# Hybrid SSD and S5 block: two token tiles scaled before a plain transpose, and two weight splits put behind them

## The chip, the cores and the metric

The kernel runs on one core of a Trainium2 chip. The metric is device time in microseconds (us) of one execution, lower is better. The kernel before takes 818.63 us (median of 3 runs, 818.24 to 820.31). The core has a matrix engine (TensorE, PE in the profile; PEld is its weight load), VectorE (DVE), ScalarE (ACT), GpSimd (POOL) and a queue engine that issues most transfers (SyncE, SP). Each engine works through its own list in order; they wait for each other on semaphores.

## The reference

One decoder block in float32 over 512 tokens with 16 learned tokens put in front (528 tokens, width 1024). What matters here is its beginning:

```python
h = jnp.concatenate([meta, x], axis=1)          # 528 x 1024
n = _rmsnorm(h, g_mix[layer])                   # h * rsqrt(mean(h*h) + eps) * g
proj = n @ w_in[layer]                          # z, xbc, dt and u side by side
...
u = proj[..., o_u:]                             # the S5 mixer's input, 1024 columns
y_s5 = _s5_mixer(u, ...)
```

Behind it follow the SSD mixer, the S5 mixer, an output projection, a squared-ReLU MLP and a last norm.

## The kernel before, in words

**Precision.** Each matrix product is made of three products of split operands: a value is cast to a short form (`whi`, `xhi`, ScalarE) and the rest is kept as a second short value (`wlo`, `xlo`). `mm_cols` (L139) runs 24 matmuls for one weight of 128 columns: for each of the 8 blocks of 128 rows of the weight, `whi`·`xhi`, `whi`·`xlo` and `wlo`·`xhi`.

**The start.** The 528 tokens come as 16 learned ones and four tiles of 128 (`xt`, t = 0 to 3). `norm_transpose_split` handles one tile: ScalarE squares and sums a row (L149), VectorE and GpSimd make `rstd` (L150, L152), and TensorE turns the tile round so that features lie on partitions. It does this with eight ordinary float32 matmuls whose moving operand is a diagonal matrix of `rstd` (`diag`, L170 and L174), so that norm and turn are one step. VectorE multiplies each half of the turned tile (four blocks, h = 0 and 1) by the gain (L176), ScalarE casts it (`xhi`, L179) and VectorE subtracts (`xlo`, L180). A small ring of three buffers (`xgs`) carries the halves between these steps.

**The first products.** `u_split(f)` splits the weight of the f-th 128 columns of u, `u_half(f, i)` multiplies it with the first (i = 0) or second half of the tokens, 264 tokens each. The first half of the tokens is the 16 learned ones, tile 0 and all but 8 tokens of tile 1. `dt_half` does the same for 16 further columns (`pd`, L271). For f = 0 and 2 VectorE makes `wlo` (L118). For f = 1 ScalarE writes the negative of the weight (L121), and a transfer that GpSimd issues adds the weight onto it (L122), before ScalarE casts `whi` (L123). Three raw buffers and three pairs of split buffers go round, so the split for f = 3 starts when the second product of f = 0 is done.

**Behind it.** ScalarE copies the turned S5 constants (`lcol`, L306), from which VectorE works out exponentials and angles in a long string of small instructions; then come the S5 blocks, the SSD chunks, the projections and the MLP. The MLP works in four quarters of 28 units; a unit of its first product is one of seven named products (P1 to P7, `Quarter.up`), several of which share a bank of accumulators (`UP_BANK`, L1070: P1, P6, P7 and P4 use bank X).

**What sets the order.** The kernel is written as a sequence of calls; a scheduler orders them on each engine by a simulated time line, by data dependences and by priorities (weights are loaded and split with a high priority). A change at one place can therefore exchange neighbours at another.

Of the kernel before, what the change touches and what calls it, by code (L numbers as in the profile page):

```python
# [10 lines left out]
F32 = mybir.dt.float32  # L11
# [3 lines left out]
ALU = mybir.AluOpType  # L15
# [3 lines left out]
P = 128  # L19
SEQ = 512  # L20
NM = 16
# [17 lines left out]
AHEAD = 3000  # L39
# [6 lines left out]
def bc(ap, axis, n):  # L46
    a = ap.unsqueeze(axis)
    shape = list(a.shape)
    shape[axis] = n
    return a.broadcast_to(shape)  # L50
# [3 lines left out]
def hybrid_block_kernel(ctx, tc, x, meta_tokens, g_mix, w_in, conv_w, conv_b, dt_bias, a_log, d_ssd,  # L54
                        g_ssd, lam_re, lam_im, log_step, b_re, b_im, c_re, c_im, d_s5, w_glu, b_glu,
                        g_s5, w_out, g_mlp, w_up, w_down, g_final, out, dbg=None):
    nc = tc.nc
    V, A, G, T = nc.vector, nc.scalar, nc.gpsimd, nc.tensor
# [20 lines left out]
    def bank(name, dt=F32):  # L79
        tag = KIND.get(name, "x")  # L80
        return ps.tile([P, 512], dt, tag=tag, name=name, bufs=TAGS[tag])

    def slot(name, shape, dt=F32):
        return big.tile(shape, dt, tag="slot", name=name)


    ident = const.tile([P, P], F32, name="ident")
# [21 lines left out]
    def split_weight(raw, lo_engine=None, ahead=AHEAD, room=None):  # L109
        with (tc.high_priority(offset=ahead) if ahead else nullcontext()):  # L110
            if room is None:
                hi = wp.tile(list(raw.shape), F32R, tag="hi", name="whi", bufs=3)
                lo = wp.tile(list(raw.shape), F32R, tag="lo", name="wlo", bufs=3)
            else:
                hi, lo = room("whi", list(raw.shape)), room("wlo", list(raw.shape))
            if lo_engine is V:
                A.copy(hi, raw)  # L117
                V.tensor_tensor(out=lo, in0=raw, in1=hi.bitcast(F32), op=ALU.subtract)  # L118
            else:

                A.mul(lo, raw, -1.0)  # L121
                G.dma_start(out=lo.bitcast(F32), in_=raw, accum_op=ALU.add)  # L122
                A.copy(hi, raw)  # L123
        return hi, lo

    def load_cols(w, c0, n=P, ahead=AHEAD):
        return load_weight(w[:, c0:c0 + n].rearrange("(k p) c -> p k c", p=P), KD, n, ahead)
# [18 lines left out]
    def rstd_of(src, n, name):  # L146
        junk = scr[:, 3]
        v = mid.tile([P, 1], F32, tag="ssq", name="ssq")
        A.activation(out=junk[:n], in_=src, func=AF.Square, accum_out=v[:n])  # L149
        V.tensor_scalar(out=v[:n], in0=v[:n], scalar1=1.0 / DM, scalar2=EPS, op0=ALU.mult, op1=ALU.add)  # L150
        r = mid.tile([P, 1], F32, tag="rstd", name=name)
        last_pow.append(G.tensor_tensor(out=r[:n], in0=v[:n], in1=mhalf[:n, 0:1], op=ALU.pow))  # L152
        return r
# [8 lines left out]
            A.copy(hi, src_p)  # L162
            V.tensor_tensor(out=xlo[:, 4 * h:4 * h + 4, c0:c0 + n], in0=src_p, in1=hi.bitcast(F32), op=ALU.subtract)

    def norm_transpose_split(src, n, gcol, xhi, xlo, c0):

        r = rstd_of(src, n, "rstd")
        m = next(turn) % 3
        diag = scr[:, 1, 640 + m * P:640 + (m + 1) * P]
        last_xn.append(A.mul(diag[:n, :n], ident[:n, :n], r[:n, 0:1]))  # L170
        for h in range(2):
            pt = bank("pt")
            for k in range(4):
                T.matmul(pt[:, k * n:(k + 1) * n], lhsT=src[:, (4 * h + k) * P:(4 * h + k + 1) * P], rhs=diag[:n, :n])  # L174
            xg = xgs[:, next(xturn) % 3, 0:4 * n].rearrange("p (k n) -> p k n", k=4)
            V.tensor_tensor(out=xg, in0=pt[:, 0:4 * n].rearrange("p (k n) -> p k n", k=4),  # L176
                            in1=bc(gcol[:, 4 * h:4 * h + 4], 2, n), op=ALU.mult)
            hi = xhi[:, 4 * h:4 * h + 4, c0:c0 + n]
            A.copy(hi, xg)  # L179
            V.tensor_tensor(out=xlo[:, 4 * h:4 * h + 4, c0:c0 + n], in0=xg, in1=hi.bitcast(F32), op=ALU.subtract)  # L180

    s5_ctx = tc.tile_pool(name="s5", bufs=1)
    s5 = s5_ctx.__enter__()
    scr = slot("scr", [P, 4, DM])
    mt = scr[0:NM, 2]
    xgs = scr[:, 0:2].rearrange("p a (h c) -> p (a h) c", h=2)
    turn, xturn = itertools.count(), itertools.count()
    last_pow, last_xn = [], []
    xt = slot("xt", [P, 4, DM])
    xhi = slot("xhi", [P, KD, L], F32R)  # L190
    xlo = slot("xlo", [P, KD, L], F32R)
# [16 lines left out]
    gcol = const.tile([P, KD], F32, name="gcol")  # L208
# [37 lines left out]
    uw, uts = {}, {}  # L246

    def u_split(f):
        raw = first_raw[f] if f in first_raw else load_cols(w_in[0], O_U + f * P)
        uw[f] = split_weight(raw, V if f in (0, 2) else G, 0 if f < 3 else AHEAD)  # L250
        uts[f] = s5.tile([P, TS5, NC5], F32, tag="ut", name="ut", bufs=2)

    def u_half(f, i):
        pu = bank("pu")
        mm_cols(pu[:, 0:LH], uw[f], xx, P, halves[i])
        A.copy(uts[f][:, :, 66 * i:66 * i + 66], pu[:, 0:LH].rearrange("p (c t) -> p t c", t=TS5))
        if i == 1:
            dma2(out=Ud[f], in_=uts[f])
# [14 lines left out]
        return A.copy(dtT[:, halves[i]], pd[0:2 * NH, 0:LH])  # L273

    def prepare(t):
        norm_transpose_split(xt[:, t], P, gcol, xhi, xlo, NM + t * P)

    norm_transpose_split(mt, NM, gcol, xhi, xlo, 0)
    prepare(0)
    u_split(0)  # L280
    prepare(1)
    prepare(2)
    u_half(0, 0)
    prepare(3)
    u_split(1)
    u_half(1, 0)
    dt_split()
    dt_half(0)
# [145 lines left out]
    for part, (x0, x1, op) in enumerate(((bRt, bIt, ALU.subtract), (bIt, bRt, ALU.add))):  # L434
# [3 lines left out]
                        in1=tb2.rearrange("p (b j) h -> p b j h", b=8), op=op)  # L438
# [10 lines left out]
        A.copy(WW[:, :, fam, 2], WW[:, :, fam, 0])  # L449

    for f in range(2, 8):
        u_split(f)
        for i in range(2):
            u_half(f, i)

# [231 lines left out]
    def xbc_tile(f):  # L687
        return xcr[:, f] if f < 8 else bcr[:, f - 8]
# [22 lines left out]
    for n, f in enumerate(order):  # L711
        raw = xbc_tile(f)
# [22 lines left out]
    for ch in range(NCH):  # L735
        n = NM if ch == 0 else P
# [15 lines left out]
        if ch > 0:  # L752
# [20 lines left out]
            for h in range(2):  # L773
# [8 lines left out]
                for r in range(4):  # L782
# [6 lines left out]
                                op=ALU.mult)  # L789
# [134 lines left out]
    for f in range(8):  # L924
        A.activation(out=yhi[:, f], in_=xc[:, f, NM:L], func=AF.Copy, scale=col("gssd", f))
        V.scalar_tensor_tensor(out=ylo[f // 2][:, f % 2], in0=xc[:, f, NM:L], scalar=col("gssd", f),
                               in1=yhi[:, f].bitcast(F32), op0=ALU.mult, op1=ALU.subtract)
# [522 lines left out]
```

## Time and profile before

| what | value |
|---|---|
| median of 3 runs | 818.63 us |
| profiled execution, its own time | 819.08 us |
| its span, first to last instruction | 817.4 us |
| TensorE busy | 774.6 us, 95% of the span |
| VectorE busy | 625.9 us, 77% |
| ScalarE busy | 496.3 us, 61% |
| GpSimd busy | 75.5 us, 9% |

The rows of a time line give the start of an instruction and its length in us, the engine, the line of the kernel, the operation, out<-in by the names of the program, partitions x elements, a count where rows are merged, and in brackets how long the engine stood idle before it and what ended that. Rows of a table of stretches give, for a stretch A:B, the busy time and instructions of each engine, then the clock that TensorE was granted, the share of the transfer engines, and GB/s. One float32 matmul of a tile's turn shows as two records. Durations overlap a little: the spacing of starts is what one instruction costs in a sequence.

### The profile page before, as it was taken

Reading aid. Unit: us, or ns where it says so; the run is one execution under the profiler, and the core shown is the slowest. Engines: PE = TensorE matmul, PEld = TensorE weight load, DVE = VectorE, ACT = ScalarE, POOL = GpSimd, SP = SyncE. Lnnn points to the kernel's source line nnn. Section 1 sums busy time; section 2 is a strip of 40 time slices with the busy share of each in tenths; the row PEclk is TensorE's granted clock in tenths of the full one; section 3 lists DMA queues with packets and bytes.
Section 4 is the critical chain, followed back from the end, with each engine's and each line's share of the span. In section 5 each row is a group of like instructions: output and inputs, shape, how many; then the busy total and the mean of one; then the engine's idle time right before and its main releaser. Section 6 shows DMA issues by size and latency. Waiting matters only on the chain. (4 is left out here: it accounts for less than half of the span.)

```text
span 817.4 us, 12922 instructions
## 1 busy us (share of the span) xinstructions
PE 774.6 (95%) x4943; PEld 682.0 (83%) x4943; DVE 625.9 (77%) x972; ACT 496.3 (61%) x782; POOL 75.5 (9%) x125
## 2 busy tenths in 40 slices
PE   6999899999999999989999989999999999999996
PEld 6999898998787778768888879878997899789975
DVE  4489798998785779769534588698679867987897
ACT  7578798988544753555123475654665466546665
POOL 3211000011000110010100000100010001000101
PEclk9999999999999999999999999999999999999998
DMA  9999575768664654344335028864485448654622
GB/s 242 194 232 217 113 167 138 172 141 190 144 154 133 163 131 132 104 125 160 123 103 186 21 78 244 192 155 156 129 181 155 156 130 181 180 159 112 117 51 104
DMA packets 129638, 121.90 MB, mean 149 GB/s; under 512 B 21836, under 2 KB 105720, under 8 KB 129576
## 3 DMA queue, kind: packets, MB, share of 16 engines
q1 hardware_dynamic: 121224, 90.66, 37.7%
q0 software_dynamic: 8352, 30.41, 20.4%
q8 instruction: 39, 0.64, 0.3%
q14 instruction: 23, 0.19, 0.1%
HBM read 83.76 MB, written 6.88 MB: 111 GB/s over the span
## 5 line engine op out<-in xcount | busy, mean ns | idle before, releaser
L997 DVE TENSOR_TENSOR wlo<-quad,whi 128x1024 fp32r<-128x1024 f32 x40 | 49.0, 1224 | 37.1 <-ACT whi L1012 34.5
L1232 PE MATMUL u<-opC,whi 128*128 128x256 f32 x384 | 71.5, 288 | 3.0 <-DVE r L99 2.0
L1012 ACT CAST whi<-quad 128x1024 fp32r<-128x1024 f32 x40 | 41.9, 1048 | 49.3 <-DMA quad<-raw 17.3
L1273 PE MATMUL acc<-whi,al 128*128 128x512 f32 x160 | 63.4, 396 | 3.7 <-DVE al L997 3.7
L1232 PEld LDWEIGHTS u<-opC,whi 128*128 128x128 f32 x384 | 60.6, 195 | 4.6 <-DVE r L99 2.6
L117 ACT CAST whi<-raw 128x1024 fp32r<-128x1024 f32 x31 | 32.3, 1043 | 52.6 <-PE acc L837 31.6
L118 DVE TENSOR_TENSOR wlo<-raw,whi 128x1024 fp32r<-128x1024 f32 x31 | 37.9, 1222 | 31.8 <-ACT whi L117 31.2
L1273 PE MATMUL acc<-whi,ah 128*128 128x512 f32 x160 | 59.6, 393 | 1.4 <-ACT ah L1012 1.4
L1273 PE MATMUL acc<-wlo,ah 128*128 128x512 f32 x160 | 60.3, 390 | 0.0
L139 PE MATMUL pxb<-xhi,whi 128*128 128x264 f32 x192 | 55.3, 288 | 1.6 <-ACT xcr L695 1.6
L139 PE MATMUL pxb<-xhi,wlo 128*128 128x264 f32 x192 | 55.8, 291 | 0.0
L139 PE MATMUL pxb<-xlo,whi 128*128 128x264 f32 x192 | 55.5, 289 | 0.0
L1232 PE MATMUL u<-opC,wlo 128*128 128x256 f32 x192 | 54.0, 286 | 0.0
L1012 ACT CAST whi<-bquad 128x1024 fp32r<-128x1024 f32 x34 | 35.7, 1049 | 30.0 <-PE acc L1273 20.8
L1232 PE MATMUL u<-opB,whi 128*128 128x256 f32 x256 | 48.6, 288 | 1.2 <-DVE opB L997 1.2
L1232 PE MATMUL u<-opA,whi 128*128 128x256 f32 x256 | 46.7, 280 | 0.2 <-ACT whi L1012 0.2
L997 DVE TENSOR_TENSOR wlo<-bquad,whi 128x1024 fp32r<-128x1024 f32 x34 | 41.5, 1221 | 3.2 <-ACT whi L1012 3.2
L1232 PEld LDWEIGHTS u<-opB,whi 128*128 128x128 f32 x256 | 40.8, 194 | 1.6 <-DVE opB L997 1.4
L1273 PEld LDWEIGHTS acc<-whi,al 128*128 128x128 f32 x160 | 30.0, 188 | 13.4 <-DVE al L997 7.5
L1232 PEld LDWEIGHTS u<-opA,whi 128*128 128x128 f32 x256 | 39.5, 188 | 0.6 <-ACT whi L1012 0.4
L1232 PE MATMUL u<-opB,wlo 128*128 128x256 f32 x128 | 37.1, 290 | 2.4 <-DVE wlo L997 2.4
L122 POOL DMA_DIRECT2D wlo<-raw x26 | 22.3, 856 | 179.2 <-ACT xcr L695 62.0
(435 smaller groups left out, 2429.0 us busy)
## 6 DMA issues: line engine op xcount, KB each, us to landing
raw<-in_w_in_dram SPq DMA_DIRECT2D x28, 512.0 KB, 4.2
wlo<-raw POOLq DMA_DIRECT2D x26, 512.0 KB, 5.2
raw<-in_w_up_dram SPq DMA_DIRECT2D x22, 512.0 KB, 4.2
raw<-in_w_glu_dram SPq DMA_DIRECT2D x16, 512.0 KB, 4.0
raw<-in_w_out_dram SPq DMA_DIRECT2D x16, 512.0 KB, 4.2
bquad<-in_w_down_dram SPq DMA_DIRECT2D x16, 512.0 KB, 3.6
quads<-in_w_down_dram SPq DMA_DIRECT2D x16, 512.0 KB, 4.4
bquad<-quads POOLq DMA_DIRECT2D x16, 512.0 KB, 5.1
```

The costliest lines, as they stand in the source:

```text
L117: A.copy(hi, raw)
L118: V.tensor_tensor(out=lo, in0=raw, in1=hi.bitcast(F32), op=ALU.subtract)
L122: G.dma_start(out=lo.bitcast(F32), in_=raw, accum_op=ALU.add)
L139: T.matmul(ps_out, lhsT=w[a][:, k, 0:m], rhs=x[b][:, k, tok], start=(n == 0), stop=(n == len(steps) - 1))
L997: V.tensor_tensor(out=out, in0=a, in1=b, op=ALU.subtract)
L1012: A.copy(hi, src)
L1232: T.matmul(pb[:, mm], lhsT=w[a][:, k, mm * P:(mm + 1) * P], rhs=x[:, b, k], start=(first and n == 0), stop=(n in (11, 23)), skip_group_che ...
L1273: T.matmul(banks[s], lhsT=at[x][:, g, j, s * P:(s + 1) * P], rhs=wt[y][:, j], start=(fresh and g == 0 and j == 0 and k == 0), stop=(g == 1 ...
```

## The change

Tiles 0 and 1 are scaled in place by ScalarE (`A.mul(src, src, r)`, 128 x 1024), and turned by TensorE's plain transpose with the identity. The learned tokens and tiles 2 and 3 keep the diagonal matrix. The second weight (f = 1) gets its low part from VectorE instead of from the transfer. The splits of f = 1 and of f = 2 to 7 are ordered behind the last parts (`xhi` and `xlo` of h = 1) of tile 1.

```diff
-    def norm_transpose_split(src, n, gcol, xhi, xlo, c0):
+    def norm_transpose_split(src, n, gcol, xhi, xlo, c0, scaled=False):
         r = rstd_of(src, n, "rstd")
-        m = next(turn) % 3
-        diag = scr[:, 1, 640 + m * P:640 + (m + 1) * P]
-        last_xn.append(A.mul(diag[:n, :n], ident[:n, :n], r[:n, 0:1]))
+        if scaled:
+            last_xn.append(A.mul(src, src, r[:n, 0:1]))
+        else:
+            m = next(turn) % 3
+            diag = scr[:, 1, 640 + m * P:640 + (m + 1) * P]
+            last_xn.append(A.mul(diag[:n, :n], ident[:n, :n], r[:n, 0:1]))
         for h in range(2):
             pt = bank("pt")
             for k in range(4):
+                if scaled:
+                    T.transpose(pt[:, k * n:(k + 1) * n], src[:, (4 * h + k) * P:(4 * h + k + 1) * P], ident[:n, :n])
+                    continue
                 T.matmul(pt[:, k * n:(k + 1) * n], lhsT=src[:, (4 * h + k) * P:(4 * h + k + 1) * P], rhs=diag[:n, :n])
...
-            A.copy(hi, xg)
-            V.tensor_tensor(out=xlo[:, 4 * h:4 * h + 4, c0:c0 + n], in0=xg, in1=hi.bitcast(F32), op=ALU.subtract)
+            last_parts[:] = [A.copy(hi, xg),
+                             V.tensor_tensor(out=xlo[:, 4 * h:4 * h + 4, c0:c0 + n], in0=xg, in1=hi.bitcast(F32),
+                                             op=ALU.subtract)]
...
-        uw[f] = split_weight(raw, V if f in (0, 2) else G, 0 if f < 3 else AHEAD)
+        uw[f] = split_weight(raw, V if f < 3 else G, 0 if f < 3 else AHEAD)
...
-        norm_transpose_split(xt[:, t], P, gcol, xhi, xlo, NM + t * P)
+        norm_transpose_split(xt[:, t], P, gcol, xhi, xlo, NM + t * P, scaled=t < 2)
...
     prepare(1)
+    second = list(last_parts)
     prepare(2)
     u_half(0, 0)
     prepare(3)
-    u_split(1)
+
+    with tc.issue_after(second[0].ins), tc.issue_after(second[1].ins):
+        u_split(1)
...
     for f in range(2, 8):
-        u_split(f)
+        with tc.issue_after(second[0].ins), tc.issue_after(second[1].ins):
+            u_split(f)
```

How the lists of the engines move is seen at three places. The first is ScalarE at the start, from the square of tile 1 on; before:

```order
L149 ACTIVATE scr,ssq<-xt 128x1024
L170 ACTIVATE scr<-ident,rstd 128x128
L117 CAST whi<-raw 128x1024
L170 ACTIVATE scr<-ident,rstd 128x128
L179 CAST xhi<-scr 128x4x16
L149 ACTIVATE scr,ssq<-xt 128x1024
L179 CAST xhi<-scr 128x4x16
L121 ACTIVATE wlo<-raw 128x1024
L123 CAST whi<-raw 128x1024
L170 ACTIVATE scr<-ident,rstd 128x128
L117 CAST whi<-raw 128x1024
L179 CAST xhi<-scr 128x4x128
```

and with the change:

```order
L149 ACTIVATE scr,ssq<-xt 128x1024
L170 ACTIVATE xt<-xt,rstd 128x1024
L117 CAST whi<-raw 128x1024
L170 ACTIVATE xt<-xt,rstd 128x1024
L186 CAST xhi<-scr 128x4x16
L149 ACTIVATE scr,ssq<-xt 128x1024
L186 CAST xhi<-scr 128x4x16
L186 CAST xhi<-scr 128x4x128
L174 ACTIVATE scr<-ident,rstd 128x128
L186 CAST xhi<-scr 128x4x128
L149 ACTIVATE scr,ssq<-xt 128x1024
L186 CAST xhi<-scr 128x4x128
```

Two diagonals became two scalings of a whole tile, and the three instructions on the weights of f = 1 and 2 left this place; the casts of tile 0 come in their stead.

The second is VectorE at the same time, from the first half of tile 0 (`scr<-pt` with 512 elements is the gain); before, and then with the change:

```order
L176 TENSOR_TENSOR scr<-pt,gcol 128x512 x2
L118 TENSOR_TENSOR wlo<-raw,whi 128x1024
L301 COPY lrow<-lsr 32x128
L180 TENSOR_TENSOR xlo<-scr,xhi 128x4x128
L176 TENSOR_TENSOR scr<-pt,gcol 128x512
L150 TENSOR_SCALAR ssq<-ssq 128x1
L266 TENSOR_TENSOR wdt_parts<-scr,wdt_parts 128x8x16
L176 TENSOR_TENSOR scr<-pt,gcol 128x512
L180 TENSOR_TENSOR xlo<-scr,xhi 128x4x128 x2
```

```order
L183 TENSOR_TENSOR scr<-pt,gcol 128x512 x2
L187 TENSOR_TENSOR xlo<-scr,xhi 128x4x128
L312 COPY lrow<-lsr 32x128
L150 TENSOR_SCALAR ssq<-ssq 128x1
L183 TENSOR_TENSOR scr<-pt,gcol 128x512
L187 TENSOR_TENSOR xlo<-scr,xhi 128x4x128
L274 TENSOR_TENSOR wdt_parts<-scr,wdt_parts 128x8x16
L187 TENSOR_TENSOR xlo<-scr,xhi 128x4x128
L183 TENSOR_TENSOR scr<-pt,gcol 128x512
L118 TENSOR_TENSOR wlo<-raw,whi 128x1024 x2
```

In the second piece the first two gains are those of tile 1; tile 0's gains and its first `xlo` stand ahead of it. The low part of one weight stood between tile 0's gains and its `xlo`; now the low parts of two weights stand behind the whole of tile 1.

The third is far from the edit: ScalarE in the first quarter of the MLP, about 495 us into the span. Before, and then with the change (`r<-u` copies an accumulator bank: L1242 and its later number L1254 is P5, L1244 and L1256 is P6; `r<-r` with two instructions is a squared ReLU):

```order
L1244 COPY r<-u 128x2x256
L1012 CAST whi<-quad 128x1024
L1073 ACTIVATE r<-r 128x2x256
L1074 ACTIVATE r<-r 128x2x256
L1012 CAST whi<-quad 128x1024
L1073 ACTIVATE r<-r 128x2x256
L1074 ACTIVATE r<-r 128x2x256
L1073 ACTIVATE r<-r 128x2x256
L1074 ACTIVATE r<-r 128x2x256
L1012 CAST whi<-quad 128x1024
L1012 CAST whi<-raw 128x1024
```

```order
L1024 CAST whi<-quad 128x1024
L1256 COPY r<-u 128x2x256
L1024 CAST whi<-quad 128x1024
L1085 ACTIVATE r<-r 128x2x256
L1086 ACTIVATE r<-r 128x2x256
L1085 ACTIVATE r<-r 128x2x256
L1086 ACTIVATE r<-r 128x2x256
L1024 CAST whi<-quad 128x1024
L1024 CAST whi<-raw 128x1024
L1085 ACTIVATE r<-r 128x2x256
L1086 ACTIVATE r<-r 128x2x256
```

The P6 copy now stands behind a cast, and the two casts at the end stand ahead of the third squared ReLU. On SP the raw loads of f = 4 (between the two constants `c_re` and `c_im`) moved behind `c_im`; the rest of SP's list is the same but for one exchange of neighbours.

More of the change, by code (lines that the diff above doesn't have):

```diff
@@ L187, in hybrid_block_kernel @@
     turn, xturn = itertools.count(), itertools.count()
-    last_pow, last_xn = [], []
+    last_pow, last_xn, last_parts = [], [], []
     xt = slot("xt", [P, 4, DM])
```

## The prediction

> **What bounds the kernel now.** I read the page's busy line first, then the table of stretches over the start, then the time line of the first 40 us, and last the places further on whose order moved.
>
> ```profile
> PE 774.6 (95%) x4943; PEld 682.0 (83%) x4943; DVE 625.9 (77%) x972; ACT 496.3 (61%) x782; POOL 75.5 (9%) x125
> ```
>
> TensorE works 774.6 of the 817.4 us of the span, so a change that leaves its long products alone can only shorten the 43 us in which it stands idle or does preparation. The change works in the first 30 us.
>
> ```profile
> 10.00:15.00 5.00, 5.00 (x30) 4.96 (x31) 3.17 (x7) 4.68 (x9) 1.64 (x2) 1.00 1.16 291
> 15.00:20.00 5.00, 4.22 (x37) 3.88 (x36) 4.78 (x10) 4.00 (x9) 2.07 (x3) 1.00 0.87 187
> 20.00:25.00 5.00, 5.00 (x45) 4.99 (x44) 4.92 (x9) 2.51 (x5) 3.02 (x5) 1.00 0.86 95
> 25.00:30.00 5.00, 5.00 (x44) 4.84 (x43) 0.54 (x2) 1.08 (x3) 0.00 (x0) 1.00 1.03 178
> ```
>
> The fourth field is VectorE: from 15 to 25 us it is full (4.78 and 4.92 of 5), then idle. TensorE has no hole after 20 us, but what it does until then is turning tiles. The time line shows when the products begin:
>
> ```profile
> 7.19 3.59 PE L174 MATMUL pt<-scr 16*128 16x16 f32 x16 [4.62 <-ACT scr L170]
> ...
> 10.71 7.00 PE L174 MATMUL pt<-scr,xt 128*128 128x128 f32 x48
> ...
> 18.48 0.51 PE L139 MATMUL pu<-xhi,whi 128*128 128x264 f32 x2 [0.78 <-ACT xhi L179]
> ...
> 18.98 2.05 PE L174 MATMUL pt<-scr,xt 128*128 128x128 f32 x16
> ...
> 20.78 0.37 PE L139 MATMUL pu<-xlo,whi 128*128 128x264 f32 x1
> ...
> 28.26 0.28 PE L139 MATMUL pu<-xhi,whi 128*128 128x264 f32 x1
> ...
> 8.21 0.39 ACT L170 ACTIVATE scr<-ident,rstd 128x128 f32<-128x128 f32 x1
> ...
> 8.83 1.04 ACT L117 CAST whi<-raw 128x1024 fp32r<-128x1024 f32 x1 [0.24 <-DMA raw<-in_w_in_dram]
> ...
> 10.24 1.06 ACT L149 ACTIVATE scr<-xt 128x1024 f32<-128x1024 f32 x1
> ...
> 11.96 1.06 ACT L121 ACTIVATE wlo<-raw 128x1024 fp32r<-128x1024 f32 x1 [0.28 <-DMA raw<-in_w_in_dram]
> 12.93 1.03 ACT L123 CAST whi<-raw 128x1024 fp32r<-128x1024 f32 x1
> ...
> 15.62 1.06 ACT L149 ACTIVATE scr<-xt 128x1024 f32<-128x1024 f32 x1
> ...
> 9.91 1.23 DVE L118 TENSOR_TENSOR wlo<-raw,whi 128x1024 fp32r<-128x1024 f32 x1 [0.58 <-ACT whi L117]
> ...
> 12.82 0.69 DVE L176 TENSOR_TENSOR scr<-pt,gcol 128x512 f32<-128x512 f32 x1 [0.88 <-PE pt L174]
> ...
> 15.22 1.22 DVE L118 TENSOR_TENSOR wlo<-raw,whi 128x1024 fp32r<-128x1024 f32 x1 [0.36 <-ACT whi L117]
> ...
> 16.37 0.21 DVE L301 COPY lrow<-lsr 32x128 f32<-32x128 f32 x1
> ...
> 16.50 0.67 DVE L180 TENSOR_TENSOR xlo<-scr,xhi 128x512 fp32r<-128x512 f32 x1
> ...
> 18.57 1.27 DVE L180 TENSOR_TENSOR xlo<-scr,xhi 128x512 fp32r<-128x512 f32 x2
> ```
>
> Tiles 0 to 2 are turned by 17.7, but the products run steadily only from 20.78. The pair of `xlo` at 18.57 is tile 0's second half and tile 1's first; the latter ends at 19.84, and tile 3's turn (18.98 to 20.78) covers that wait. From 20.78 to 28.26 stand 61 of the 64 matmuls of the first token half (24 + 24 for u, 16 for dt), 0.12 us each; at 28.26 the second half begins. So **VectorE's string of gains and low parts, 0.60 us each, sets the start**, and my yardstick is when that second half begins.
>
> **The change, part by part.** *ScalarE.* The diagonal (0.39) becomes a pass over 1024 elements, which costs what the other passes of that size do, 1.06, spaced 0.97 (11.96 to 12.93). From 8.21: scaling to 9.17, cast of the first weight to 10.13 (it was at 8.83), second scaling to 11.1, the square of tile 2 from 11.25 instead of 10.24. That is 1.0 late, and the pair at 11.96 and the cast behind it, three passes of 0.97, are gone before 15 us, so ScalarE is ahead from there on. The square of tile 3 could come at 14.1; its load had landed by 15.62, no row tells when before. If only then, ScalarE is 1.5 later, tile 1's cast ends near 17.3, and the products start 0 to 0.5 later; I take 0, since no wait stands before 15.62.
>
> *TensorE.* Sixteen plain transposes replace sixteen float32 matmuls of two records each. Warm prices: 16 records of tile 3 took 1.80 from start to start; twelve transposes of this kind stand further on:
>
> ```profile
> 36.44 1.53 PE L443 MATMUL pc<-ident,scr 128*128 128x128 f32 x12
> ...
> 10.00:14.00 4.00, 4.00 (x21) 3.96 (x22) 2.48 (x6) 3.68 (x8) 1.28 (x2) 1.00 1.15 317
> 14.00:18.00 4.00, 3.70 (x34) 3.51 (x32) 3.47 (x8) 3.66 (x8) 0.43 (x2) 1.00 0.95 173
> ```
>
> 0.12 each, against 0.23 for a matmul. But until about 14 us TensorE is slow: 21 records in 4.00 us, then 34 in 3.70, though the granted clock reads 1.00 in both. A slow transpose has no row; bounds are 0.12 (the warm row) and 0.20 (the slow pace of one record). I take 0.20, as they stand at 10.7 to 14: 16 cost 3.2, and tiles 0 and 1 are round at 14.0 instead of about 15.8. Half of tile 0 is ready at 11.9 instead of 12.82; tile 2's matmuls follow until 15.9.
>
> *VectorE.* The first weight's low part goes from 9.91 to 10.25, ending 11.4. Gains of tile 0 at 11.9 and 12.7, `xlo` of the learned tokens, `xlo` at 13.5, gains of tile 1 at 14.0 and 14.6, `xlo` at 15.2 to 15.8. No weight stands between: the 1.22 at 15.22 went behind tile 1. Then the copy at L301; it needs a load that had landed by 16.37, so it costs 0 to 0.6 of waiting; I take 0.2. One gain of tile 2 (0.60), and the `xlo` of tile 1's first half ends at about 17.5 (19.84 before).
>
> *First token half.* Products run from 17.5. In the new order tile 3's turn (1.80) lies within them: 63 x 0.121 + 1.80 = 9.4, so the second half begins at 26.9 against 28.26: **-1.35**. The 2.3 us that VectorE wins shrink to this because the turn used to fill the wait. The two low parts (18.8 to 21.1) and tile 3's gains and low parts end near 25.6, so the second token half, at 26.9, is covered by 1.3; without that cover each us late there costs one. Bounds: -2.8 if TensorE never waits (transposes and tile 2 done at 15.9, then 64 x 0.121 and 1.80), 0 if VectorE's late low parts stop TensorE for all of it.
>
> *Left out and moved.* One GpSimd transfer and its ScalarE pass go; they lay beside the turning, worth 0 alone. The f = 4 load on SP slips behind two constants:
>
> ```profile
> 27.27 0.53 SPq L106 DMA_DIRECT2D raw<-in_w_in_dram  x1
> ...
> 27.90 1.18 SPq L293 DMA_DIRECT2D scr<-in_c_im_dram  x1
> ...
> DMA to landing us min/median/max: 3.8/5.2/6.3
> ...
> 34.22 1.05 ACT L123 CAST whi<-raw 128x1024 fp32r<-128x1024 f32 x1 [0.70 <-ACT ut L256]
> ...
> 36.78 0.21 ACT L306 COPY lcol<-pl 128x96 f32<-128x96 f32 x1
> ...
> 54.07 0.19 DVE L375 TENSOR_TENSOR cs<-cs 128x32 f32<-128x32 f32 x1 [2.44 <-ACT cs L374]
> ```
>
> Issued some 2.5 later, near 29.8, it lands after 3.8 to 6.3 (these loads' own row), at 33.6 to 36.1. Its cast is wanted at 32.9 and holds ScalarE's `lcol` behind it: median 35.0, so `lcol` comes at 37.6, 0.8 late. VectorE's constants behind it have 2.44 of slack before ScalarE's sine, less the 1.35 by which that comes earlier: 1.1, enough. Cost 0, bound +0.8 at the longest landing.
>
> *MLP.* Here nothing was edited, only the order moved.
>
> ```profile
> 495.36 0.59 ACT L1244 COPY r<-u 128x512 f32<-128x512 f32 x1 [4.03 <-PE u L1232]
> ...
> 496.69 1.05 ACT L1012 CAST whi<-quad 128x1024 fp32r<-128x1024 f32 x1 [0.75 <-DMA quad<-raw]
> ...
> 497.74 0.39 PE L1232 MATMUL u<-opC,whi 128*128 128x256 f32 x2
> ...
> 506.67 1.23 DVE L997 TENSOR_TENSOR wlo<-quad,whi 128x1024 fp32r<-128x1024 f32 x1 [1.17 <-ACT whi L1012]
> ...
> 507.64 0.50 PE L1232 MATMUL u<-opC,whi 128*128 128x256 f32 x2 [0.44 <-ACT whi L1012]
> ...
> 522.12 0.75 PE L1232 MATMUL u<-opC,whi 128*128 128x256 f32 x2 [1.95 <-DVE r L99]
> ...
> 480.00:500.00 20.00, 15.91 (x116) 15.16 (x115) 17.64 (x20) 12.39 (x18) 0.90 (x1) 0.91 0.44 110
> ```
>
> The P6 copy now waits behind the cast (end 497.64 + 0.59 = 498.2), and P7 at 497.74 uses its bank: +0.5. The casts ahead of the third squared ReLU fill VectorE's 1.17 idle, 0.65 of it by the time its moved `r` takes, and with it the 0.44; the chain of transfers that ends the 1.95 starts 0.65 earlier. At 522 the latter decides. Bounds -1.17 and +0.5; I take **-0.4**, nearer the chain that ends last.
>
> **Sum:** -1.35 - 0.4 = -1.75 on 819.08 (817.4 of span and 1.7 around it) is 817.3. The profiled run is 0.45 above the median, so I forecast 816.9 for the median.
>
> **Rivals.** *Slow clock.* If plain transposes do not bring TensorE to its fast pace, tile 2's 16 records run at 0.19 and end at 17.1, still hidden; but products from 17.5 on may run at half speed for one more spell. The row with 0.91 shows how long such a spell is: 9% of 20 us lost, 3.6 us at half, a loss of 1.8. Total -1.75 + 1.8: 818.7, no change. For: the fast pace came only after matmuls of full tiles, not in the 3.59 us of the learned tokens. Against: transposes keep TensorE as full. The Trainium skill ("TensorE: Matmul & The Clock Gate", Part 4: PE-mode transpose) states that transposes do not count as busy for the clock gate as matmuls do; by it this rival holds, at 818.7. No row here shows it either way.
>
> *Swallowed.* VectorE's late string or `lcol` takes the 1.35 back: 818.2 to 818.7. For: VectorE is the full engine at 15 to 25. Against: 1.3 and 1.1 of cover.
>
> *MLP stall (slower).* The P6 copy now hangs on the transfer that ends the 0.75 wait. Each us that it lands later than 496.65 stops P7 as long. A stop of 3 us, with a slow spell behind it as in the 0.91 row (1.8), gives -1.35 + 3 + 1.8 = +3.4: 822.1. It decides from a landing 1.3 later on. Against: its issue follows VectorE's string, which isn't moved there.
>
> *More than forecast.* TensorE waits half as long as I say and the MLP gains 1.1: -2.1 - 1.1 = -3.2: 815.4. For: slow transposes at 0.12 free the gains earlier. Against: VectorE's string is the limit either way.
>
> **How the numbers follow.** Forecast 0.45, slow clock 0.17, swallowed 0.14, stall 0.10, more 0.14. What this kernel's measurement tells from no change is about 0.3%, 2.5 us: faster means under 816.2, slower over 821.1. The forecast, give or take 1.2, puts 0.27 of its 0.45 under 816.2 (0.12), the last case nearly all its 0.14; slow clock and swallowed are "same"; the stall is slower, with 0.01 from elsewhere. Faster 0.26, same 0.63, slower 0.11. The range, 8 in 10, takes in the neighbours but not the stall: 814.9 to 819.8.
>
> **What would show it.** Right: `xlo` of tile 1's first half ends near 17.5, no products before it but one, tile 3's turn within the products, second half at 26.9, `lcol` between 36 and 38, u's last products 1.3 earlier, TensorE's 1.95 near 522 down by 0.6. Wrong: products at double spacing after 17.5 (slow clock), a wait of TensorE for `xlo` near 25, `cs` released by its own chain and not by ScalarE, a stop of TensorE at 497.

## The result, and the profile after

The changed kernel takes 824.17 us (median of 7 runs, 822.81 to 829.09), the kernel before, run between, 819.61 (818.24 to 820.46): a ratio of 1.0071 with a 95% interval of 1.0049 to 1.0093. I had forecast 816.9; it is slower by 0.7%. The profiled execution took 829.09 us, the slowest of the seven, so its trace shows more than the median's loss.

The page of the changed kernel, its line of busy times and its line of code loads (packets, MB, share of the transfer engines' time):

```profile
PE 777.7 (94%) x4927; PEld 685.6 (83%) x4927; DVE 628.0 (76%) x973; ACT 496.5 (60%) x781; POOL 75.4 (9%) x124
...
q8 instruction: 39, 0.64, 0.3%
```

TensorE has 16 matmuls and 16 weight loads fewer than before (4943 each), since a plain transpose is one of each and a diagonal float32 product two. The second line I had read past: 39 transfers of 16 KB that carry code. Both lines turn out to belong together.

The start, in the time line of the changed kernel:

```profile
10.68 3.67 PE L179 MATMUL pt<-ident,xt 128*128 128x128 f32 x16
...
14.14 2.02 PE L181 MATMUL pt<-scr,xt 128*128 128x128 f32 x16
...
15.19 1.06 ACT L149 ACTIVATE scr<-xt 128x1024 f32<-128x1024 f32 x1 [0.89 <-DMA xt<-in_x_dram]
...
17.16 0.68 DVE L187 TENSOR_TENSOR xlo<-scr,xhi 128x512 fp32r<-128x512 f32 x1
...
17.89 0.39 PE L139 MATMUL pu<-xlo,whi 128*128 128x264 f32 x1 [0.61 <-DVE xlo L187]
...
22.12 1.95 PE L181 MATMUL pt<-scr,xt 128*128 128x128 f32 x16
...
27.42 0.28 PE L139 MATMUL pu<-xhi,whi 128*128 128x264 f32 x1
27.64 0.31 PE L315 MATMUL pl<-ident,lrow 32*128 32x32 f32 x2
...
35.34 1.05 ACT L123 CAST whi<-raw 128x1024 fp32r<-128x1024 f32 x1 [2.17 <-DMA raw<-in_w_in_dram]
...
37.78 0.22 ACT L317 COPY lcol<-pl 128x96 f32<-128x96 f32 x1
...
53.56 0.19 DVE L386 TENSOR_TENSOR cs<-cs 128x32 f32<-128x32 f32 x1 [0.91 <-ACT cs L385]
```

The start did roughly what was forecast, at smaller size: the second token half begins at 27.42 instead of 28.26, and the constants arrive 0.5 us earlier than before (53.56 against 54.07). The loss is further on. If one matches the instructions of TensorE by name and order in both traces, the changed kernel's start less the earlier one, as a median over stretches, is:

| place, us | 40 to 60 | 100 to 140 | 170 to 200 | 210 to 240 | 250 to 350 | 370 to 500 | 530 to 560 | end |
|---|---|---|---|---|---|---|---|---|
| difference, us | -0.5 | -0.3 | +1.2 | +4.8 | +5.1 to +5.6 | +6.8 | +10.4 | +10.1 |

So there are four steps. The table of stretches of the changed kernel has the granted clock as the third number from the right:

```profile
160.00:180.00 20.00, 17.58 (x144) 16.98 (x143) 17.82 (x31) 16.25 (x31) 2.57 (x3) 0.91 0.66 155
200.00:220.00 20.00, 16.22 (x99) 13.46 (x98) 12.65 (x24) 11.74 (x17) 1.72 (x2) 0.91 0.63 140
360.00:380.00 20.00, 17.28 (x78) 13.04 (x77) 11.59 (x19) 9.38 (x22) 1.09 (x1) 0.83 0.31 85
...
520.00:540.00 20.00, 15.73 (x94) 14.77 (x93) 10.42 (x11) 11.75 (x16) 3.30 (x4) 0.83 0.83 183
```

and the same table of the kernel before:

```profile
160.00:180.00 20.00, 17.58 (x156) 17.06 (x155) 18.89 (x33) 17.77 (x32) 2.55 (x3) 1.00 0.69 160
200.00:220.00 20.00, 18.35 (x114) 15.24 (x113) 16.10 (x31) 13.96 (x21) 2.51 (x3) 1.00 0.73 172
360.00:380.00 20.00, 18.20 (x106) 14.56 (x105) 16.35 (x28) 9.93 (x19) 0.00 (x0) 0.91 0.22 79
...
520.00:540.00 20.00, 17.51 (x80) 14.64 (x80) 18.30 (x20) 13.00 (x16) 4.25 (x5) 0.91 0.67 132
```

At each step a spell of half clock (granted 0.50 from 209 to 212 us) is new or twice as long: 9% of 20 us is one of some 3.4 us, 17% two, and one costs about 1.7 us. Two of the steps also have a wait of TensorE that is over 2 us longer; at a third, near 365 us, a wait for VectorE's `S` grew from 1.8 to 2.7. The waits of TensorE in the kernel before (us in total, times, longest):

```profile
PE u L1232 <- DVE r L99: 2.0, 1, 2.0
PE py L594 <- DMA Tp<-Kd: 1.7, 1, 1.7
```

and in the changed one:

```profile
PE py L606 <- DMA Tp<-Kd: 5.7, 3, 3.8
...
PE u L1244 <- DVE r L99: 4.3, 1, 4.3
```

The first, near 205 us, is for the third Toeplitz block of the S5 scan, which goes out to memory (`Kd`) and comes back (`Tp`); the second, near 526 us, is in the MLP, where the scheduler had exchanged neighbours. Nothing that the change edited stands at either place.

### The profile page after: what moved, and what is told of

Same layout as the page of the kernel before. It is cut to its first block, busy times and chain, and to the rows that moved or that the text cites. A ratio compares the mean times of both kernels' runs of the same rounds, so it can differ in the third digit from the quotient of the medians.

```text
span 827.4 us, 12888 instructions
## 1 busy us (share of the span) xinstructions
PE 777.7 (94%) x4927; PEld 685.6 (83%) x4927; DVE 628.0 (76%) x973; ACT 496.5 (60%) x781; POOL 75.4 (9%) x124
## 5 line engine op out<-in xcount | busy, mean ns | idle before, releaser
L1244 PE MATMUL u<-opC,whi 128*128 128x256 f32 x384 | 72.1, 290 | 6.2 <-DVE r L99 4.3
L1244 PEld LDWEIGHTS u<-opC,whi 128*128 128x128 f32 x384 | 61.2, 197 | 7.2 <-issue 4.4
L117 ACT CAST whi<-raw 128x1024 fp32r<-128x1024 f32 x32 | 33.3, 1043 | 53.9 <-PE acc L849 31.6
L1244 PE MATMUL u<-opC,wlo 128*128 128x256 f32 x192 | 54.2, 288 | 0.0
L1244 PE MATMUL u<-opB,whi 128*128 128x256 f32 x256 | 48.0, 286 | 1.2 <-DVE opB L1009 1.2
L1244 PE MATMUL u<-opA,whi 128*128 128x256 f32 x256 | 46.9, 281 | 0.2 <-ACT whi L1024 0.2
L1244 PEld LDWEIGHTS u<-opB,whi 128*128 128x128 f32 x256 | 40.4, 193 | 1.4 <-DVE opB L1009 1.4
L1244 PEld LDWEIGHTS u<-opA,whi 128*128 128x128 f32 x256 | 39.8, 189 | 0.6 <-ACT whi L1024 0.4
L123 ACT CAST whi<-raw 128x1024 fp32r<-128x1024 f32 x25 | 26.1, 1044 | 22.9 <-PE pz L139 10.9
L1244 PE MATMUL u<-opB,wlo 128*128 128x256 f32 x128 | 36.9, 288 | 2.4 <-DVE wlo L1009 2.4
```

The costliest lines, as they stand in the source:

```text
L1244: T.matmul(pb[:, mm], lhsT=w[a][:, k, mm * P:(mm + 1) * P], rhs=x[:, b, k], start=(first and n == 0), stop=(n in (11, 23)), skip_group_che ...
```

## The experiments

The expectations call the MLP's first products "the gated layer", and the experiments' "small products" are 8x8 matmuls of the identity into unused columns of a bank. All ratios are to the kernel before, run in between on the same chip; its median was 819.6 to 820.5 in the four sessions, so kernels of different sessions are compared by their ratios (0.001 is 0.8 us).

**The parts of the change, one by one.** Four kernels, against the changed one:

```diff
 a1, the turn alone
-        uw[f] = split_weight(raw, V if f < 3 else G, 0 if f < 3 else AHEAD)
+        uw[f] = split_weight(raw, V if f in (0, 2) else G, 0 if f < 3 else AHEAD)
 a1, a2 and a3, no hold (both places)
-    with tc.issue_after(second[0].ins), tc.issue_after(second[1].ins):
-        u_split(1)
+    u_split(1)
 a2 and a4, no plain turn
-        norm_transpose_split(xt[:, t], P, gcol, xhi, xlo, NM + t * P, scaled=t < 2)
+        norm_transpose_split(xt[:, t], P, gcol, xhi, xlo, NM + t * P, scaled=False)
```

> Tiles 0 and 1 scaled and turned as in the change, but the second weight's low part stays on ScalarE and a GpSimd accumulate, and no split is held back. Behind the start this kernel issues its instructions in the order of the kernel before, in the scan over the blocks and in the gated layer alike. Theory A (the loss of the changed kernel comes from what the scheduler put in another order further down, and from the weight loads that run at other times there): 818.5 to 819.5, the early 0.3 to 0.5 us kept, ratio 0.999 to 1.000. Theory B (the clock's slow spells come where the start shifts by some tenths of a us, whatever is moved): as the changed kernel, 822 to 826. Theory C (the turn by transposes itself costs): above 822 too, and then the two that keep diagonal products are at 819.6.

> Only the second weight's low part goes to VectorE; all tiles are scaled by the diagonal products, no split is held back. One accumulate fewer on GpSimd's queue; the gated layer has the order of the kernel before. Theory A: 819 to 821, and if the wait for the Toeplitz block's transfers near 205 us in the changed kernel comes from this accumulate, 821.5 to 822.5 with that wait of some 4 us in its trace. Theory B: 822 to 826. Theory C: 819.6.

> The turn by transposes and the split on VectorE, but no split held back: the order in the gated layer (the sixth product's copy behind a cast) is the changed kernel's, the order of the loads in the first 40 us is not (the fifth weight stays ahead of the second table). Theory A, if the order in the gated layer is the larger part: 822 to 825; if the load behind the table is it: 819 to 820. Theory B: 822 to 826. Theory C: as the turn alone.

> The split on VectorE and the hold, but all tiles by diagonal products: the order in the gated layer is that of the kernel before, and the fifth weight's load stands behind the second table, as in the changed kernel. Theory A, if the load behind the table is the larger part: 822 to 825; if the order in the gated layer is it: 819 to 820.5. Theory B: 822 to 826. Theory C: 819.6.

Measured: the turn alone 826.09 us, ratio 1.0083 (1.0050 to 1.0116); the split on VectorE alone 819.66, 0.9998 (0.9976 to 1.0020); no hold 822.21, 1.0034 (1.0010 to 1.0059); the weights alone 820.15, 0.9994 (0.9973 to 1.0015). Theory A as I had put it falls: the kernel with the turn alone issues everything behind the start in the old order, and is the slowest of the four. The two that keep the diagonal products lose nothing beyond the noise, as theory C says; but the transposes stand in the first 15 us and the step is near 205. Theory B falls as well: a2 shifts the start by 0.3 us and a4 by -0.8, and neither is near 822. What reaches from the transposes to 205 us?

**Code loads.** The transfers of the third block stand behind a weight load on SP's queue, which stands behind a transfer that adds `raw` onto `wlo`. The transfers of the kernel before at 190 to 194 us (queue 8 carries code; the last number of the lower row is from issue to landing):

```profile
q8 instruction: 1, 0.02, 1.9%
...
wlo<-raw POOLq DMA_DIRECT2D x1, 512.0 KB, 4.7
```

and of the changed kernel at 194 to 198 us:

```profile
q8 instruction: 1, 0.02, 1.4%
...
wlo<-raw POOLq DMA_DIRECT2D x1, 512.0 KB, 6.0
```

Before, a code load of TensorE starts at 191.9 us, 1.9 ahead of the accumulate's issue (193.8), which then takes 4.7 us. In the changed kernel it starts at 195.5, 0.5 behind the issue (195.0), and the accumulate takes 6.0. What follows in the changed kernel's time line:

```profile
200.97 0.38 SPq L106 DMA_DIRECT2D raw<-in_w_in_dram  x1
...
201.13 0.86 POOL L122 DMA_DIRECT2D wlo<-raw  x1 [5.33 <-ACT wlo L121]
201.44 3.07 SPq L553 DMA_DIRECT2D Tp<-Kd  x4
...
208.93 0.77 PE L606 MATMUL py<-ub,Tp 128*128 128x128 f32 x2 [3.78 <-DMA Tp<-Kd]
```

and in that of the kernel before:

```profile
198.55 0.38 SPq L106 DMA_DIRECT2D raw<-in_w_in_dram  x1
199.02 1.96 SPq L541 DMA_DIRECT2D Tp<-Kd  x4
...
205.64 0.46 PE L594 MATMUL py<-ub,Tp 128*128 128x128 f32 x2 [1.65 <-DMA Tp<-Kd]
```

The weight load waits for the accumulate, the block's transfers for the weight load; now the next accumulate (201.13) is issued ahead of all four instead of behind the first two (199.97 before), and their issue alone takes 3.07 instead of 1.96. TensorE waits 2.1 longer, and a slow spell follows: the step of 3.6. The Trainium skill ("Runtime: NRT & Kernel Launch", Instruction fetch mechanics) says that an engine's code is refilled in blocks of 16 KiB, 256 instructions, by a transfer queue of its own, at a cost that is mostly hidden. The size agrees (39 loads for 2 x 4927 matmuls and weight loads, and 40 in b3 below, which has 224 more than the kernel before). The load at 195.5 us is not hidden; what the other 38 cost no run here shows. Theory D follows: 32 instructions fewer at the start move the later code loads against the work. It was tested by putting 32 instructions back where TensorE is idle, and by taking the kernel before to the same remainder of 256:

```diff
-    T.transpose(pgr[:, 0:KD], grow, ident[:KD, :KD])
+    T.transpose(pgr[:, 0:KD], grow, ident[:KD, :KD]); [T.matmul(pgr[0:8, 16:24], lhsT=ident[0:8, 0:8], rhs=ident[0:8, 0:8]) for _ in range(8)]
```

(8 in b1 to the turn alone, b2 to the change and b4 to the kernel before; 56 in b3.)

> The turn alone, and ahead of the first turn eight 8x8 products of the identity whose result nobody reads: they are 16 matmuls and 16 weight loads, as many instructions as the sixteen plain transposes have fewer than the diagonal products, in time in which TensorE waits for x. Theory D (code loads): TensorE's code is 32 instructions shorter with the transposes, its code is loaded at other moments from then on, and one of these loads, at 198.0 us instead of 191.9, meets the transfers ahead of the scan's third Toeplitz block. With the 32 put back the load falls ahead of them again: the wait for the block near 207 us goes from 3.2 to 1.7 us, the accumulate ahead of it from 5.9 to 4.8 us, and the time from 826.1 to 819 to 822 (the rest is the slow clock spell at 17 us that the turn alone had). Theory B (clock spells by the shift of the start) and theory C (the transposes themselves): 824 to 827, the wait stays.

> The whole change with the same eight small products ahead. Theory D: the code loads of TensorE stand where they stood before, the accumulate at 195 us takes 4.8 instead of 6.0 us, the wait for the third block is 1.7 to 1.9 instead of 3.8 us, no slow spell follows it, and the time is 819 to 821.5; what is above 819 is the other order in the gated layer. Theories B and C: as the change, 823 to 826.

> The kernel before with 56 of the small products: 224 instructions more, which is 32 fewer modulo 256, the 16 KB of one code load, so that the code loads stand at about the places that they have in the kernel with the turn, and nothing else of it is changed. Theory D: the accumulate ahead of the third block at about 6 us, the wait for the block 3 to 4 us, 822 to 826. Theories B and C: 819.6 plus what the products push the first turn back, under 1 us.

> The kernel before with eight of the small products: 32 instructions more, code loads 2 to 3 us earlier against the work. It tells what the small products cost by themselves and what another position gives. Theory D: a time of its own, between 817 and 823, that its code loads explain, with the third block's wait at 1.7 us if the load at 192 us moves to 189. Theories B and C: 819 to 820.

Measured: 821.22 (1.0012, 0.9998 to 1.0027), 821.17 (1.0009, 0.9991 to 1.0027), 824.20 (1.0058, 1.0037 to 1.0080) and 816.81 (0.9963, 0.9946 to 0.9980). Eight products that nobody reads take 0.0071 (5.8 us) off the ratio of the turn alone and 0.0062 (5.1 us) off that of the change, with all transposes still in place, so theory C falls; 56 of them give the kernel before the change's wait. Only b4 came out better than any theory had it (817 to 823). The kernel before with 56, at 194 to 198 us:

```profile
q8 instruction: 1, 0.02, 1.5%
...
wlo<-raw POOLq DMA_DIRECT2D x1, 512.0 KB, 5.8
```

and its wait is 3.55 us. The matched difference of b3 goes from +3.4 to +6.9 there, as in the change; a further 2.7 it lost at the start, where I expected under 1, to the products themselves and a slow spell at 20 us. The change with eight has its code load back ahead, at 192.5; at 194 to 198 us it shows:

```profile
wlo<-raw POOLq DMA_DIRECT2D x1, 512.0 KB, 4.9
```

**More places, and the order in the MLP.** c1 and c4 put sixteen of the products ahead, in the change and in the kernel before. c2 and c3 hold back a sum and a weight's split in the MLP, so that P6's copy and P2's subtraction stand ahead again (c2 with 8 products ahead, c3 with 16):

```diff
-            vadd(b["S"], b[1, 0], b[1, 1])
+            with (tc.issue_after(p2c[2].ins) if self.q == 0 and self.g == 1 else nullcontext()): vadd(b["S"], b[1, 0], b[1, 1])
...
-                self.w[i] = split_w(self.cols[g].get(m))
+                with ExitStack() as es:
+                    [es.enter_context(tc.issue_after(x.ins)) for x in (p6c[0:1] + p2c[3:4] if self.q == 0 and i == 7 else ())]
+                    self.w[i] = split_w(self.cols[g].get(m))
```

(`p2c` holds P2's subtractions and squares, `p6c` P6's copies.)

> The whole change with sixteen of the small products: against the kernel before its code on TensorE is 32 instructions longer, as in the kernel before with eight of them, which took 816.8 us. Theory D: the place of the code loads sets most of the time, so 816 to 818.5 us. Rival (only the load near the third block matters, which eight had mended): 820.5 to 822, as with eight.

> The change with eight small products, and in the first quarter of the gated layer the order of the kernel before put back: the sixth product's copy and the second product's subtraction of the second group ahead of the cast and the sum that had gone in front of them; the third squared ReLU stays two casts later. If that order costs what the changed kernel's trace had at 520 to 530 us (a wait of 4.3 us for VectorE instead of 2.0, and a slow spell of 6.8 instead of 3.4 us): 818 to 820 against 821.2 without it. If the order costs nothing: 821 to 821.5.

> Both: sixteen small products and the order of the gated layer put back. It is the candidate to beat both kernels: theory D with the order costing 2 us gives 814 to 817, theory D with the order costing nothing 816 to 818.5, the rival of the run before it 818 to 821.

> The kernel before with sixteen small products, 64 instructions more: what the next place of the code loads gives. Theory D has no sign here, only that it can differ from the 819.6 of none and the 816.8 of eight by more than 1 us, up to 824; if code loads mattered at the third block alone it is 817 to 820 with its wait at 1.7 to 2.1 us.

Measured: 818.66 (0.9977, 0.9956 to 0.9998), 818.42 (0.9972, 0.9951 to 0.9992), **816.04 (0.9953, 0.9931 to 0.9975)** and 820.18 (0.9999, 0.9978 to 1.0019). c1 lies between theory D (816 to 818.5) and its rival (820.5 to 822): more than the one load matters, but its order in the MLP still costs. c4 is 0.6 us from the 819.6 that I had named, less than the 1 us that I had set. By the ratios the order costs 0.0037 (3.0 us) with eight products (b2 against c2) and 0.0024 (2.0 us) with sixteen (c1 against c3), each give or take some 2.3. Where it costs is near 525 us. The changed kernel:

```profile
504.23 1.05 ACT L1024 CAST whi<-quad 128x1024 fp32r<-128x1024 f32 x1 [6.08 <-DMA quad<-raw]
...
505.18 0.58 ACT L1256 COPY r<-u 128x512 f32<-128x512 f32 x1
...
527.30 1.23 DVE L99 TENSOR_TENSOR quad<-bquad 128x1024 f32<-128x1024 f32 x1 [4.24 <-DMA bquad<-in_w_down_dram]
528.45 1.22 DVE L1009 TENSOR_TENSOR wlo<-raw,whi 128x1024 fp32r<-128x1024 f32 x1
529.58 0.68 DVE L99 TENSOR_TENSOR r<-u,r 128x512 f32<-128x512 f32 x1
...
530.41 0.77 PE L1244 MATMUL u<-opC,whi 128*128 128x256 f32 x2 [4.27 <-DVE r L99]
```

the kernel before, whose wait of 1.95 at 522.12 the prediction shows:

```profile
516.10 1.22 DVE L997 TENSOR_TENSOR wlo<-raw,whi 128x1024 fp32r<-128x1024 f32 x1
520.24 1.23 DVE L99 TENSOR_TENSOR quad<-bquad 128x1024 f32<-128x1024 f32 x1 [2.93 <-DMA bquad<-in_w_down_dram]
521.38 0.68 DVE L99 TENSOR_TENSOR r<-u,r 128x512 f32<-128x512 f32 x1
```

and a3:

```profile
500.55 1.05 ACT L1024 CAST whi<-quad 128x1024 fp32r<-128x1024 f32 x1 [5.47 <-DMA quad<-raw]
501.50 0.58 ACT L1256 COPY r<-u 128x512 f32<-128x512 f32 x1
...
519.27 1.22 DVE L1009 TENSOR_TENSOR wlo<-raw,whi 128x1024 fp32r<-128x1024 f32 x1
522.65 1.23 DVE L99 TENSOR_TENSOR quad<-bquad 128x1024 f32<-128x1024 f32 x1 [2.17 <-DMA bquad<-in_w_down_dram]
523.80 0.68 DVE L99 TENSOR_TENSOR r<-u,r 128x512 f32<-128x512 f32 x1
...
524.54 0.50 PE L1244 MATMUL u<-opC,whi 128*128 128x256 f32 x2 [1.14 <-DVE r L99]
```

TensorE waits for an `r` that VectorE makes behind a sum (`quad<-bquad`), and the sum waits for its transfer. Before, VectorE made the low part of the next weight (`wlo<-raw`) ahead of that sum, in time in which it would have waited; now the low part stands between the sum and `r`, which comes 1.14 us later for it. Besides, four `acc` products that TensorE did just ahead of the wait (from 519.08, some 0.9 us) come behind it (from 535.67), and the transfer took 6.49 instead of 6.31. Together that is 2.2 of the 2.3 us by which the wait grew. The copy of P6 behind the cast is not the cause: a3 has it too, with ScalarE idle for 5.47 us ahead of the cast, and TensorE waits 1.14 us there and is granted 1.00 from 520 to 540. So a3 does not have the whole order of the changed kernel, as I had expected: the low part and the four products stand as before. In c2 and c3 they do as well, and the wait is 1.14 and 1.15, shorter than in the kernel before, so theirs is not the old order but a better one. In c2 the stretch has its clock again:

```profile
520.00:540.00 20.00, 18.16 (x89) 14.84 (x88) 18.44 (x21) 13.39 (x17) 3.58 (x5) 1.00 0.77 149
```

In c1 (and b2), with the changed order, it is 0.83 as in the change; in d1 below, with that order too, 0.91 and a wait of 2.8.

**Two controls.** d1 puts the eight products into the change behind the first quarter of the MLP (ahead of unit 0 of the second), so that the code up to there is as short as the change's. d2 is c2 without any small products.

> The whole change with the eight small products behind the first quarter of the gated layer instead of ahead of everything: the code ahead of the scan is as short as in the change, so its code loads up to some 620 us stand where the change has them. Theory D: the wait of 3.2 to 3.8 us for the third block and the accumulate of 5.8 to 6.0 us are there again, 823 to 826, as the change. If it were the small products themselves that help: 821 to 822.

> The change with the order of the gated layer put back and no small products. If the two causes add: 824.2 less 2.7, 821 to 822, with the wait for the third block still 3 to 4 us and no slow spell of 6.8 us at 520 to 540 us. If the order costs only where the code loads stand as with the products: 823.5 to 825.

Measured: 826.29 (1.0073, 1.0045 to 1.0102) and 821.39 (1.0010, 0.9990 to 1.0029). Products behind the scan don't help; so it is not their presence but what stands ahead of the scan. By the ratios the change loses 0.0061 (5.0 us) less with the order mended (d2), 0.0062 (5.1 us) less with the code mended (b2), and 0.0099 (8.1 us) less with both (c2); with the other mended already, the order is worth 3.0 (b2 against c2) and the code 3.1 (d2 against c2). Each difference is good to some 2.3 us. That each of the two costs is shown; how large each is, between 2 and 6 us, and whether they add exactly, is not. d2's waits show one mended and the other not:

```profile
PE py L606 <- DMA Tp<-Kd: 5.9, 3, 3.3
...
PE u L1246 <- DVE r L99: 0.5, 1, 0.5
```

All kernels at the third block (code: TensorE's instructions ahead of it against the kernel before, where +224 is -32 modulo 256; the times in us are read off the issues in each time line; the medians are of four sessions, in which the kernel before had 819.6 to 820.5):

| kernel | code | code load less issue of the accumulate | that issue to the next weight load's | wait for the block | median us |
|---|---|---|---|---|---|
| change | -32 | +0.5 | 6.0 | 3.8 | 824.2 |
| a1 turn alone | -32 | +0.8 | 5.9 | 3.2 | 826.1 |
| a3 no hold | -32 | +1.0 | 6.0 | 3.8 | 822.2 |
| d1 products late | -32 | +0.4 | 5.9 | 3.3 | 826.3 |
| d2 order back | -32 | +0.4 | 5.9 | 3.3 | 821.4 |
| b3 before, 56 | +224 | +0.6 | 5.8 | 3.6 | 824.2 |
| before | 0 | -1.9 | 4.8 | 1.7 | 819.6 |
| a2, a4 | 0 | -1.9, -2.0 | 4.9, 4.8 | 1.9, 1.7 | 819.7, 820.2 |
| b1, b2, c2 | 0 | -1.9 each | 4.9, 5.0, 4.9 | 2.0, 1.8, 1.8 | 821.2, 821.2, 818.4 |
| b4, c1, c3 | +32 | -1.8, -1.9, -1.9 | 5.0, 4.9, 4.7 | 2.1, 1.7, 1.6 | 816.8, 818.7, 816.0 |
| c4 before, 16 | +64 | -6.0 | 5.2 | 2.2 | 820.2 |

The six with the load just behind the issue, one of them the kernel before with nothing changed but its code length, have the long accumulate and a wait of over 3 us; the ten others do not. What the experiments set is the length of the code ahead of this place; that the load itself slows the accumulate is read from these sixteen rows.

**What stays open.** 32 instructions more than before (b4, c1, c3) leave the load near the third block where it was and still gain 0.0019 to 0.0037 of the ratio, 1.6 to 3.0 us, over the same kernel with 32 fewer (c3 against c2, the smallest, is within the noise); which of the other 38 loads gives that, I did not trace. And c2, the change with both faults mended, is 0.9972 (0.9951 to 0.9992) of the kernel before. Its profiled run was the fastest of its twelve (816.41), and its matched difference ends at -2.6: -0.5 from the start, +1.5 by 170 to 200 us, where a slow spell is new, then -2.3 near 365, where the kernel before has a slow spell and c2 has none, and -1.1 from there to 560 us, over the stretch with the shorter wait near 520. So most of it stands near 365 us and in the MLP, not at the start. With 32 instructions more on both sides, c3 against b4, the change is worth 0.9953 to 0.9963, 0.8 us, which is within the noise.

## Why the prediction was wrong

**The start: right in kind, too large.** "Products run from 17.5" was 17.89, "the second half begins at 26.9" was 27.42. The sixteen transposes took 3.46 from start to start, not 3.2; tile 3's square did wait for its load (0.89), which I had bounded at up to 0.5 on the products and taken at 0; tile 3's turn took no longer than forecast (at most 1.70 from start to start, against 1.80). Two small transposes of `lrow` then slipped in at 27.64. So -1.35 became -0.84 at 27.42 and -0.5 at 40 to 60 us.

**Slow clock: not in the change.** Tile 2's sixteen records took 2.02 from 14.14 and the products came 0.12 apart. But with the turn alone the rival did happen: its stretch from 0 to 20 us was granted 0.93.

```profile
0.00:20.00 20.00, 10.31 (x50) 9.97 (x51) 8.66 (x22) 16.58 (x30) 6.02 (x43) 0.93 0.84 229
```

It lost 1.6 us there against the kernel before, and b1, with a spell at the same place, 1.3. What these two have and the change has not is a wait of TensorE for ScalarE's diagonal between the transposes and tile 2's turn, 2.40 us in a1 and 2.21 in b1, with the spell right behind it:

```profile
16.80 3.31 PE L181 MATMUL pt<-scr,xt 128*128 128x128 f32 x16 [2.40 <-ACT scr L174]
```

So the rule of the Trainium skill ("TensorE: Matmul & The Clock Gate", Part 4: PE-mode transpose), by which transposes don't count as busy, is neither shown nor refuted: the same sixteen transposes had a slow spell behind them in two kernels, each time behind a wait of over 2 us, and none in the change.

**The fifth weight's load and `lcol`: right.** The cast waited 2.17 for the slipped load, `lcol` came at 37.78 (36 to 38 forecast), and VectorE still waited 0.91 for ScalarE at `cs`, so nothing was lost.

**The MLP: wrong sign.** "I take -0.4" measured +2 to +5, by the ratios of the pairs above. The step that failed is "the chain of transfers that ends the 1.95 starts 0.65 earlier. At 522 the latter decides". Where the chain starts did not decide. Counted from the end of TensorE's last stop for `wlo` (490.94 in the kernel before, 497.76 in the change, 493.25 in b2), its transfer `quad<-bquad` is issued 17.26 us later in the kernel before, 17.33 in the change and 16.68 in b2, which is the 0.6 earlier that was forecast; yet the wait is 4.27 in the change and 4.29 in b2. What decided is what stands behind the chain and beside it, which I had taken as it was: the low part between the sum and `r` (1.14) and the four products that no longer stand ahead of the wait. The forecast looked at ScalarE's order near 495 us, and the exchange that costs is VectorE's and TensorE's near 520. The stall rival, given 0.10, had the sign and nearly the price (3 + 1.8; 2.3 more of wait and one more slow spell of 1.7 in the trace), but that is luck: P7 was not stopped near 497, and P6's late copy, its cause, costs nothing in a3.

**The missing term.** Sixteen plain transposes "replace sixteen float32 matmuls of two records each", I wrote, and priced the records as TensorE's time. The term that has no place in the sum is their number: 32 instructions fewer shift code loads further on, and that measured +3 to +6 (5.1 from the change to b2, 3.1 from d2 to c2, 5.8 from a1 to b1). It could have been looked for, since the line of queue 8 was on the page, but not its size: which load meets which transfer is seen only once the kernel has run. The change lost 5.8 us by the ratio (4.0 to 7.6); without both faults it gains 2.3 (0.7 to 4.0). That this is near the forecast -1.75 is luck: the start gave 0.5 of the 1.35.

The spell at 164 us in the profiled run does not go with the change: b4 and c4, built on the kernel before, have it (0.91 from 160 to 180 us), and a3 and c1, with the transposes, do not. The doubled spell from 360 to 380 us (0.83) stands in the profile of the changed kernel alone; no other kernel has more than one spell there, and it is not explained.

## What to carry to other kernels

An edit that changes the number of instructions on one engine can move later code loads of that engine, and where a queue has transfers with a tight meeting (a load behind an accumulate behind a load) that alone can cost about half a per cent far from the edit; a few idle instructions ahead of it tell this apart from the edit's own worth. Compare the order of the whole program on every engine, not of the edited part: of the exchanges seen here, a copy put behind a cast whose weight was still on its way cost nothing (a3), and a low part put behind a sum whose transfer was still on its way cost nearly its whole length, since TensorE waited for what came next. And an edit worth under 1% should be judged at more than one place of the code: with both faults mended the change was 0.28% faster than the kernel before at the old code length, no different from it with 32 instructions more (c3 against b4), and as delivered 0.71% slower. The best version, c3, is 0.47% faster than the kernel before; the kernel before with eight idle products gets 0.37% without the change.

## What the runs showed of the hardware

At the third block a 512 KB accumulate took 5.8 to 6.0 us, up to the issue that waits for it, where a code load of 16 KB, about 1 us long, started 0.4 to 1.0 us behind its issue (6 kernels), and 4.7 to 5.2 where it started 1.8 us or more ahead (10 kernels). The place does not follow the code's length evenly: 32 instructions fewer move the load 2.3 to 2.9 us later against the work, 32 more not at all, 64 more 4.1 us earlier. All six kernels with a wait of 3.2 us or more for the third block were granted 0.91 from 200 to 220 us, and so was c4 with its 2.2; b4 with 2.1 and the kernel before with 1.65 were granted 1.00. So in these traces a wait of 2.2 us came with a slow spell of some 1.7 us behind it, nearly as much again, and one of 2.1 did not; but near 164 us one and the same wait of 2.4 us has a spell behind it in b4 and none in the kernel before.
